# Mixture of experts in one layer of a two-block network: tokens of the first two expert pairs put in order by float32 products and a gather in place of products with bf16 parts

## The chip, the cores and the metric

The kernel runs on one core of a Trainium2 chip. The metric is the device time of that core in microseconds for one execution. Names of engines: PE is TensorE, DVE is VectorE, ACT is ScalarE, POOL is GpSimd, SP is SyncE, which here only issues DMA transfers.

## The reference, cut to what matters

The network has two blocks on 512 tokens of width 1024. The first block mixes tokens (`out_proj` is its last product and adds to X), then sends each token to two of 32 experts, then adds a small gated term; the second block has an attention mixer and an MLP. The part that the change touches is the second step of the first block:

```python
h = rmsnorm(x, g_ffn)
grp_logits = h @ w_grp                     # 4 groups, the best one is taken
exp_logits = h @ w_exp                     # 8 experts in each group, the best two of that group
gate = softmax(top two logits) * p_group
for each expert e:                         # on the tokens that chose e
    y = (silu(xb @ w1[e]) * (xb @ w3[e])) @ w2[e]
x = x + sum over a token's two experts of gate * y
```

Every expert has 1024x512 weights w1 and w3 and 512x1024 weights w2, in float32: 6 MB for an expert.

## The kernel before

**Pairs.** The 32 experts are worked off as 16 pairs. A pair has 128 places, 64 for each expert. `experts` runs over the pairs: the tokens of a pair stand turned in a tile xT (width on the partitions, places along the row), products L1090 and L1091 (one expert in each half of the array's columns) give w1's and w3's results (`up`, tile pa), then come the gate function, four transposes (pact), the products with w2 (py, L1179 and L1180) and the products that add the pair's result to X (pc, L1102). The next pair's w1 (`up(xs[0], True, turn)`) stands between a pair's w3 and its transposes, so that PE has work while DVE and ACT compute.

**Weights.** The weights come as 192 tiles of 1 MB by SP's queue (L670), 12 tiles for a pair. Each tile goes to a slot; the slots are used in turn, and a slot is loaded again when its products are done. At first 12 slots are loaded while `out_proj` and the router run: four `rg`, three `we`, the slot `hs[3]` and four of the ring; after the router seven more, three of `mg` and four of the ring. The slots `hs[1:3]` join the row after the first pair's w3, when the parts of X that they hold are no longer read. That makes 21.

**Order of tokens.** A pair's tokens are picked out by a matrix O of zeros and ones (token by place, bf16), which DVE makes from the places (L996, L997). There are two ways to xT:

- For the first two pairs the product of X and O gives xT directly (`add`, L1002, tile pxT). X is float32, so it is cut into three bf16 parts (`split3`, lines L175 to L183, in the slots `hs[0:3]`), and each of 4 token tiles x 8 blocks of the width takes three bf16 products: 96 for a pair. The first pair's products run while the router finishes (`first`): tiles 0 to 2 before, tile 3 last, since it needs the router's last places. The second pair's are done in two halves of 48 (`go`), one after the first pair's w1 and one after its w3.
- For the other pairs `fetch` multiplies O by the token's numbers and norms (tile pr, L1046), makes a list of rows from that on DVE (rsl, idx) and lets POOL gather these rows of X from DRAM (L1019, an indirect DMA from xd into xg, which lies in the slot `hs[0]` and is set to zero once by POOL, L1130). `go` then turns the gathered rows with eight transposes (L1033). The rows of X are written to xd by ACT's queue while the router runs.

**Router.** `Router.tile` runs for each of 4 token tiles beside the second half of `out_proj`: transposes of X (trp), logits (pl), a long row of small DVE operations for the best experts (lg to Mb), a count of places before this tile (pp), then slot and O. Tile 3's chain stands behind the last product of `out_proj`.

**Order of instructions.** A scheduler lists the instructions of each engine before the run, by priorities (`issue_after` holds back) and its own estimates. Engines then run their lists in order and wait for each other by semaphores.

Of the kernel before, what the change touches and what calls it, by code (L numbers as in the profile page):

```python
# [18 lines left out]
P = 128  # L19
# [667 lines left out]
def moe(N, a, mg, mixed):  # L687
# [4 lines left out]
    with ExitStack() as ctx:  # L692
# [53 lines left out]
        rtags = [(rg, "r%d" % i, 1) for i in range(4)]  # L746
        tags = [(we, "e%d" % i, 1) for i in range(3)]
        ring = [(N.ring, "w", RING)] * RING
        first = rtags[1:2] + rtags[:1] + rtags[2:] + tags + N.hs[3:] + ring[4:]
        W = Weights(N, a, first, [(0, NE)])  # L750
        H = [slot_tile(s, BF, (NT, D)) for s in N.hs[:3]]
        O = small("O", [P, 2, NT, P], BF)
        router = Router(N, mo, H, wr, c)

        def loaded():
            W.fetch(len(first))

        d = Dispatch(N, [(None, O[:, 0])] * 2, c, 0, (), H)
        router.d = d
        mixed(loaded, router.tile)  # L760
        W.free = mg[:3] + ring[:4]
# [22 lines left out]

        steps = {PLE_AT + i: lambda: next(pl.steps, 0) for i in range(1, 4)}
        steps.update({-1: where, PLE_AT: embed, PLE_AT + 4: rest})
        xs, pa = experts(N, bufs, c, W, 0, 14, [d], then=steps, H=H)

        over = [s for s in W.free if s not in ring][-3:]
        W.drop(over)  # L790
# [26 lines left out]
class Router:  # L817

    def __init__(self, N, mo, H, wr, c):
        self.N, self.mo, self.H, self.wr, self.c, self.pl = N, mo, H, wr, c, None

    def half(self, t, j):

# [12 lines left out]
            nc.tensor.matmul(self.pl[:, :36], lhsT=x[:, k * P:(k + 1) * P], rhs=self.wr[:, 4 * j + k, :],  # L838
                             start=j == 0 and k == 0, stop=j == 1 and k == 3)

    def parts(self, t, j):

        h = slice(j * 512, (j + 1) * 512)
        self.N.split3([x[:, t, h] for x in self.H], self.N.X[:, t, h], t == NT - 1 and j == 1)

    def tile(self, t):
        N, nc, c = self.N, self.N.nc, self.c
        if t == 0:
            self.half(0, 0)
            self.parts(0, 0)  # L850
        self.half(t, 1)
        nc.scalar.dma_start(c["xd"][t * P:(t + 1) * P, :], N.X[:, t, :])
        r = N.rnorm(t)
        if t == NT - 1:
            self.parts(t, 1)
            self.d.first((0, 1))
            self.d.first((2,))

        def st(name, n, dt=F32):
            return self.mo.tile([P, n], dt, tag=name, bufs=2, name=name)  # L860

        i32, slot, e12, q = (c[x] for x in ("i32", "slot", "e12", "q"))
        lg, m8, x8, Mb = (c[x][:, t, :] for x in ("lg", "m8", "x8", "Mb"))
        nc.vector.tensor_scalar(lg[:, :36], self.pl[:, :36], r, None, op0=OP.mult)
        i8, gs, pen, mk, j8 = st("i8", 8, U32), st("gs", 1), st("pen", 4), st("mk", NE), st("j8", 8, U32)
        nc.vector.max(m8, lg[:, 32:40])
        nc.vector.max_index(i8, m8, lg[:, 32:40])
        nc.vector.tensor_copy(gs, i8[:, 0:1])
        nc.vector.tensor_scalar(pen, i32[:, 0:4], gs, NEG, op0=OP.not_equal, op1=OP.mult)
        nc.vector.tensor_tensor(mk.rearrange("p (g e) -> p g e", g=4), lg[:, :NE].rearrange("p (g e) -> p g e", g=4),  # L870
                                pen[:, :, None].to_broadcast([P, 4, 8]), op=OP.add)
        nc.vector.max(x8, mk)
        nc.vector.max_index(j8, x8, mk)
        e = e12[:, :, t]
        nc.vector.tensor_copy(e, j8[:, 0:2])
        M1, jk, b = st("M1", NE), st("jkr", NE), st("sb", 2)
        nc.vector.tensor_scalar(M1, i32, e[:, 0:1], None, op0=OP.is_equal)
        nc.vector.scalar_tensor_tensor(Mb, i32, e[:, 1:2], M1, op0=OP.is_equal, op1=OP.add)
        pp = N.misc("pp")[:, :NE]
        for s in range(t):  # L880
            nc.tensor.matmul(pp, lhsT=c["two"], rhs=c["Mb"][:, s, :], start=s == 0, stop=False)
        nc.tensor.matmul(pp, lhsT=c["before"], rhs=Mb, start=t == 0, stop=True)
        nc.vector.tensor_scalar(b, e, 2.0 * CAP, None, op0=OP.mult)
        for i in range(2):
            nc.vector.scalar_tensor_tensor(jk, i32, e[:, i:i + 1], pp, op0=OP.is_equal, op1=OP.mult,
                                           accum_out=q[:, i, t:t + 1])

        nc.vector.scalar_tensor_tensor(b, q[:, :, t], 2.0 * CAP, b, op0=OP.is_ge, op1=OP.add)
        nc.vector.tensor_tensor(slot[:, :, t], b, q[:, :, t], op=OP.add)
        self.d.places(t, slot)  # L890
        if t < NT - 1:
            self.parts(t, 1)
        with N.tc.issue_after(self.d.last.ins):
            N.split3([c["r"][:, t, i:i + 1] for i in range(3)], r, True)
        if t < NT - 1:
            self.half(t + 1, 0)
            self.parts(t + 1, 0)


def gating(N, rt, c):  # L900
# [75 lines left out]
class Dispatch:  # L976
# [1 line left out]

    def __init__(self, N, bufs, c, pi, ts=range(NT), H=None):
        self.N, self.H, self.c, self.n, self.ps = N, H, c, 0, None
        self.pi = pi
        self.xT, self.O = bufs[pi % len(bufs)]
        self.two = len(bufs)
        sg = c["slot"]
        if pi:
            sg = N.tmp("sg", [P, 2, NT], tag="sg", bufs=2)
            N.nc.vector.tensor_scalar(sg, c["slot"], 4.0 * CAP * pi, None, op0=OP.subtract)
        for t in ts:  # L990
            self.places(t, sg)

    def places(self, t, sg):
        nc, iot = self.N.nc, self.c["iot"]
        o1 = self.c["mo"].tile([P, P], BF, tag="o1", bufs=2, name="o1")
        nc.vector.tensor_scalar(o1, iot, sg[:, 0, t:t + 1], None, op0=OP.is_equal)  # L996
        self.last = nc.vector.scalar_tensor_tensor(self.O[:, t, :], iot, sg[:, 1, t:t + 1], o1, op0=OP.is_equal,  # L997
                                                   op1=OP.add)

    def add(self, p, k, t, start=False):  # L1000
        for i in range(3):
            self.mm = self.N.nc.tensor.matmul(p, lhsT=self.H[i][:, t, every(k)], rhs=self.O[:, t, :],  # L1002
                                              start=start and i == 0, stop=t == NT - 1 and i == 2, skip_group_check=True)

    def out(self, p, k):
        N, nc = self.N, self.N.nc
# [17 lines left out]
    def go(self):  # L1024

        p = self.N.either("pxT")
        for i in range(4):
            k = self.n + i
            if self.H:
                for t in range(NT):  # L1030
                    self.add(p[:, i * P:(i + 1) * P], k, t, t == 0 and i == 0)
            else:
                self.mm = self.N.nc.tensor.transpose(p[:, i * P:(i + 1) * P], self.xg[:, every(k)], self.N.ident)  # L1033
        for i in range(4):
            self.out(p[:, i * P:(i + 1) * P], self.n + i)
        self.n += 4
        if self.n == KD and self.H:
            self.norm()
        return self

    def norm(self):
# [22 lines left out]
            self.norm()  # L1064


def experts(N, bufs, c, W, p0, p1, xs=None, pa=None, then={}, H=None):

# [38 lines left out]
    for pi in range(p0, p1):  # L1110
# [6 lines left out]
        nxt = None  # L1117
        if two and pi == 0:
            with N.tc.issue_after(xs[0].last.ins):
                xs.append(Dispatch(N, bufs, c, 1, H=H))  # L1120
            xs[1].go()
        x = xs.pop(0)
        pa.append(up(x))
        if left:
            with tc.issue_after(x.ups[3]):
                back(*left.pop())
        if two and pi == 0:
            xs[0].go()
            c["xg"] = slot_tile(N.hs[0], F32, (2, D))
            nc.gpsimd.memset(c["xg"], 0.0)  # L1130
            W.free += N.hs[1:3]
            xs.append(Dispatch(N, bufs, c, 2).fetch())
        if -1 - pi in then:
            then[-1 - pi]()
# [639 lines left out]
```

## Time and profile before

| what | us |
|---|---|
| median of 3 runs (1829.17 to 1829.71) | 1829.69 |
| the profiled execution | 1830.18 |
| its span, first to last instruction | 1828.5 |
| PE busy in the span | 1793.8 (98%) |
| DVE, ACT, POOL busy | 857.1, 586.7, 76.0 |

The experts run from 394.5 us to about 880 us of the span. The router, beside the second half of `out_proj`, runs from about 350 us to 394.5 us. Everything after that is the gated term of the first block and the second block. The page divides the span in 40 slices; PE's slices have a 9 (90% or more) from the second to the 39th. The clock granted to PE was 0.999 of full speed on average. The DMA share of a stretch is the mean busy share of the core's 16 DMA engines.

Products of float32 tiles take two records each in the trace where both operands are plain float32 (`sp`, `pl`); a transpose takes one.

### The profile page before, as it was taken

What the parts mean: (1) busy time and instruction counts of PE and PEld (TensorE: products, weight loads), DVE (VectorE), ACT (ScalarE), POOL (GpSimd) and SP (SyncE); (2) the same over time, 40 slices, a digit from 0 to 9 for tenths busy, and PEclk for the clock granted to TensorE, in tenths of its full rate; (3) what the DMA queues carried; (4) which work ended last, traced back from release to release, by engine and by line L of the source; (5) the groups of instructions that cost most, each with busy time, mean ns of one, the idle gap of its engine ahead of it and who ended that gap; (6) DMA issues with size and microseconds to landing.
All of it is one profiled execution on the core that took longest, in us unless ns stands there. A gap on an engine that the chain in (4) does not pass through costs nothing.

```text
span 1828.5 us, 20908 instructions
## 1 busy us (share of the span) xinstructions
PE 1793.8 (98%) x8425; PEld 1240.1 (68%) x8425; DVE 857.1 (47%) x1620; ACT 586.7 (32%) x953; POOL 76.0 (4%) x136
## 2 busy tenths in 40 slices
PE   7999999999999999999999999999999999999998
PEld 5777888864443444443677668787888888888886
DVE  6565433365545445324764557555224443333333
ACT  6453322322111112111755652424223432222221
POOL 1001000100000000000020010000000000000000
PEclk9999999999999999999999999999999999999999
DMA  5122223979999997999312021212233222332221
GB/s 191 47 92 90 78 93 97 354 258 424 423 423 423 423 409 303 424 423 374 131 36 91 24 73 46 92 36 81 82 103 130 87 72 94 96 104 99 92 92 46
DMA packets 117888, 322.60 MB, mean 176 GB/s; under 512 B 8797, under 2 KB 69393, under 8 KB 93720
## 3 DMA queue, kind: packets, MB, share of 16 engines
q1 hardware_dynamic: 115192, 315.46, 45.7%
q0 software_dynamic: 2016, 3.64, 0.5%
q10 hardware_dynamic: 576, 2.10, 0.3%
q8 instruction: 68, 1.11, 0.3%
q14 instruction: 36, 0.29, 0.0%
HBM read 320.68 MB, written 4.19 MB: 178 GB/s over the span
## 4 chain that ended last, share of the span: by engine, by line
PE 46%; issue 3%; ACT 2%; DVE 1%; POOL 1%; DMA 0%; POOLq 0%; DVEq 0%; ACTq 0%
PE acc L268 7%; PE acc L269 7%; PE acc L270 7%; PE pf L270 3%; PE pf L269 3%; PE pf L268 3%; PE pg L270 2%; PE pg L268 2%; PE pg L269 2%; PE psc L1605 2%; PE pu L270 1%; PE pu L268 1%; PE pu L269 1%; PE pa L1090 1%; PE po L1505 1%
## 5 line engine op out<-in xcount | busy, mean ns | idle before, releaser
L167 DVE TENSOR_TENSOR wlo<-wraw,whi 128x1024 fp32r<-128x1024 f32 (+2 forms) x165 | 226.5, 1384 | 350.9 <-PE pg L269 107.6
L165 ACT ACTIVATE whi<-wraw 128x1024 fp32r<-128x1024 f32 (+2 forms) x169 | 193.3, 1165 | 246.6 <-DMA wraw<-in_w_ff_dram 121.4
L268 PE MATMUL acc<-wh,whi 128*128 128x512 f32 (+1 forms) x448 | 170.7, 381 | 1.7 <-ACT fq L1442 1.0
L269 PE MATMUL acc<-wh,whi 128*128 128x512 f32 (+1 forms) x448 | 170.4, 380 | 0.0
L270 PE MATMUL acc<-wh,wlo 128*128 128x512 f32 (+1 forms) x448 | 169.9, 379 | 0.0
L268 PE MATMUL acc<-whi,wh 128*128 128x512 f32 x288 | 116.2, 404 | 0.6 <-ACT wh L165 0.4
L270 PE MATMUL acc<-whi,wh 128*128 128x512 f32 x288 | 114.9, 401 | 0.9 <-DVE wh L169 0.9
L269 PE MATMUL acc<-wlo,wh 128*128 128x512 f32 x288 | 114.9, 400 | 0.2 <-POOL wlo L167 0.2
L269 PE MATMUL pg<-wh,whi 128*128 128x512 f32 x256 | 101.5, 397 | 0.0
L268 PE MATMUL pg<-wh,whi 128*128 128x512 f32 x256 | 101.3, 396 | 0.0
L270 PE MATMUL pg<-wh,wlo 128*128 128x512 f32 x256 | 101.1, 395 | 0.0
L268 PE MATMUL pf<-whi,jh 128*128 128x512 f32 x256 | 101.1, 395 | 0.0
L269 PE MATMUL pf<-wlo,jh 128*128 128x512 f32 x256 | 101.1, 395 | 0.0
L270 PE MATMUL pf<-whi,jl 128*128 128x512 f32 x256 | 101.1, 395 | 0.0
L268 PEld LDWEIGHTS acc<-wh,whi 128*128 128x128 f32 x448 | 84.5, 189 | 21.5 <-issue 1.5
L269 PEld LDWEIGHTS acc<-wh,whi 128*128 128x128 f32 x448 | 84.5, 189 | 18.0 <-issue 1.8
L270 PEld LDWEIGHTS acc<-wh,wlo 128*128 128x128 f32 x448 | 84.5, 189 | 16.5
L1104 DVE TENSOR_TENSOR X<-pc,X 128x512 f32<-128x512 f32 x128 | 80.6, 684 | 15.2 <-PE pc L1102 14.3
L1090 PE MATMUL pa<-ww,wm 128*64 128x512 f32 x176 | 80.8, 599 | 0.3 <-PEq L803 0.3
L1091 PE MATMUL pa<-ww,wm 128*64 128x512 f32 x168 | 77.3, 599 | 0.0
L1102 PEld LDWEIGHTS pc<-y,OT 128*128 128x128 f32 x256 | 44.6, 188 | 41.7 <-issue 24.1
L1102 PE MATMUL pc<-y,OT 128*128 128x512 f32 x256 | 71.0, 411 | 0.3 <-DVE X L1104 0.2
(472 smaller groups left out, 3454.5 us busy)
## 6 DMA issues: line engine op xcount, KB each, us to landing
ww<-in_w_dram SPq DMA_DIRECT2D x71, 1024.0 KB
wraw<-in_w_in_dram SPq DMA_DIRECT2D x44, 1024.0 KB
wr<-in_w_dram SPq DMA_DIRECT2D x34, 1024.0 KB
wm<-in_w_dram SPq DMA_DIRECT2D x33, 1024.0 KB
wraw<-in_w_ff_dram SPq DMA_DIRECT2D x32, 1024.0 KB
wh<-in_w_dram SPq DMA_DIRECT2D x31, 1024.0 KB
we<-in_w_dram SPq DMA_DIRECT2D x23, 1024.0 KB
wraw<-in_w_out_dram SPq DMA_DIRECT2D x8, 1024.0 KB
```

The lines of the kernel that those rows point to most:

```text
L165: nc.scalar.activation(hi, src, AF.Copy, scale=scale)
L167: (pool or nc.vector).tensor_tensor(lo, src, f32v(hi), op=OP.subtract)
L268: mm(out, lhsT=lh, rhs=rh, start=start, stop=False, **kw)
L269: mm(out, lhsT=lh, rhs=rl, start=False, stop=False, **kw)
L270: mm(out, lhsT=ll, rhs=rh, start=False, stop=stop, **kw)
L1090: nc.tensor.matmul(p[0:64], lhsT=x.xT[:, kk, :64], rhs=wt[0][:, k, :], start=kk == 0, stop=kk == 7)
L1091: x.ups.append(nc.tensor.matmul(p[64:128], lhsT=x.xT[:, kk, 64:], rhs=wt[1][:, k, :], start=kk == 0, stop=kk == 7).ins)
L1102: nc.tensor.matmul(pc, lhsT=OT[:, t * P:(t + 1) * P], rhs=y[i], start=i == 0, stop=i == 1)
L1104: nc.vector.tensor_tensor(x, pc, x, op=OP.add)
L1505: nc.tensor.matmul(po[h * 64:(h + 1) * 64, i * P:], lhsT=v[:, i, (2 * c + h) * 64:(2 * c + h + 1) * 64], rhs=w[:, h, c0:c1], start=(i == N ...
L1605: nc.tensor.matmul(pl[:, cs], lhsT=fk[:, m, cs], rhs=fq[:, m, cs], start=True, stop=True)
```

## The change

The three bf16 parts of X and their operations (`parts`, `split3` on X) go. What takes their place:

- **First pair:** `places` also casts each tile's O to float32 (O0, one DVE copy for each of the four tiles), and `add` is one product of X and O0 in float32 in place of three: 32 products where 96 stood.
- **Second pair:** its Dispatch now calls `fetch` like those of the later pairs, behind the first pair's w1: product pr, list, gather. Its eight transposes (`go().go()`) stand behind the last product of the first pair's w3 (`issue_after(x.ups[-1])`). The third pair's `fetch` follows them.
- **Slots:** `hs[1:3]` hold no parts of X any more and are among the slots loaded first: 14 then, and all 21 from the beginning. The gather's buffer in `hs[0]` and its zeroing move to the beginning of `moe`.

```diff
-        first = rtags[1:2] + rtags[:1] + rtags[2:] + tags + N.hs[3:] + ring[4:]
+        first = rtags[1:2] + rtags[:1] + rtags[2:] + tags + N.hs[1:] + ring[4:]
         W = Weights(N, a, first, [(0, NE)])
-        H = [slot_tile(s, BF, (NT, D)) for s in N.hs[:3]]
+        c["xg"] = slot_tile(N.hs[0], F32, (2, D))
+        nc.gpsimd.memset(c["xg"], 0.0)
...
-        d = Dispatch(N, [(None, O[:, 0])] * 2, c, 0, (), H)
+        d = Dispatch(N, [(None, O[:, 0])] * 2, c, 0, (), N.tmp("O0").rearrange("p (t s) -> p t s", t=NT))
...
-    def parts(self, t, j):
-
-        h = slice(j * 512, (j + 1) * 512)
-        self.N.split3([x[:, t, h] for x in self.H], self.N.X[:, t, h], t == NT - 1 and j == 1)
...
+        if self.O0 is not None:
+            nc.vector.tensor_copy(self.O0[:, t, :], self.O[:, t, :])
 
     def add(self, p, k, t, start=False):
-        for i in range(3):
-            self.mm = self.N.nc.tensor.matmul(p, lhsT=self.H[i][:, t, every(k)], rhs=self.O[:, t, :],
-                                              start=start and i == 0, stop=t == NT - 1 and i == 2, skip_group_check=True)
+        self.mm = self.N.nc.tensor.matmul(p, lhsT=self.N.X[:, t, every(k)], rhs=self.O0[:, t, :], start=start,
+                                          stop=t == NT - 1, skip_group_check=True)
...
             with N.tc.issue_after(xs[0].last.ins):
-                xs.append(Dispatch(N, bufs, c, 1, H=H))
-            xs[1].go()
+                xs.append(Dispatch(N, bufs, c, 1).fetch())
         x = xs.pop(0)
         pa.append(up(x))
...
         if two and pi == 0:
-            xs[0].go()
-            c["xg"] = slot_tile(N.hs[0], F32, (2, D))
-            nc.gpsimd.memset(c["xg"], 0.0)
-            W.free += N.hs[1:3]
+            with tc.issue_after(x.ups[-1]):
+                xs[0].go().go()
             xs.append(Dispatch(N, bufs, c, 2).fetch())
```

The lists show it at three places. The first is PE between the last product of `out_proj` (acc) and the products of token tile 3; pp is the count of places (tile 3's are the last four), two and before are its matrices. Before, the products of tiles 0 to 2 are bf16 with a load of weights for each, and run on past the count for tile 2; this is a piece of that list:

```order
L1002 LDWEIGHTS wh_2387
L1002 MATMUL pxT<-O,wh_2387 128x128
L882 LDWEIGHTS before
L882 MATMUL pp<-Mb,before 128x32
L1002 LDWEIGHTS wh_2388
L1002 MATMUL pxT<-O,wh_2388 128x128
```

With the change, the same stretch in whole:

```order
L876 MATMUL pp<-Mb,before 128x32
L270 MATMUL acc<-whi,wm_1515 128x512
L994 MATMUL pxT<-O_2389,X 128x128 x4
L832 MATMUL trp<-ident,X 128x128 x4
L994 MATMUL pxT<-O_2389,X 128x128 x5
L839 MATMUL pl<-wr,xr 128x36 x4
L994 MATMUL pxT<-O_2389,X 128x128 x15
L875 LDWEIGHTS two
L875 MATMUL pp<-Mb,two 128x32
```

The 72 bf16 products between the last acc and tile 3's count have become 24 float32 ones, and the count for tile 2 now stands ahead of the last acc.

The second place is PE from the first pair's w3 to the second pair's w1 (L1090 and L1091 before, L1075 and L1076 now). Before, 48 bf16 products stand in front of w3 and 48 more behind it; this is the piece at w3's end:

```order
L1091 MATMUL pa<-wh_2540,wm_3040 64x512
L1090 MATMUL pa<-we_2538,wm_3040 64x512
L1091 MATMUL pa<-wh_2540,wm_3040 64x512
L1002 LDWEIGHTS wh_2386
L1002 MATMUL pxT<-O,wh_2386 128x128
L1002 LDWEIGHTS wh_2387
```

With the change (wh_2386 is the gather's buffer; the four pr between w1 and w3, not shown, feed the gather's list):

```order
L1076 MATMUL pa<-wh_2540,wm_2960 64x512
L1021 MATMUL pxT<-ident,wh_2386 128x128 x8
L1032 LDWEIGHTS O
L1032 MATMUL pr<-r,O 128x6
...
L917 MATMUL pm<-ident,qm 1x128
L1075 MATMUL pa<-wh_2542,wm_2960 64x512
L957 MATMUL sp<-ident,slot 128x128 x8
```

Eight transposes of the gathered rows stand where 48 products stood, and nothing but four pr stands between w1 and w3.

The third place is SP's list at the end of the mixer, a piece of the difference: the slots `hs[1]` and `hs[2]` are loaded (wh_2540 and wh_2542 here are `hs[1]` and `hs[2]` now, and wh_2540 was `hs[3]` before), the first of them ahead of the third tile of `out_proj`'s weights.

```order
-L252 DMA wraw<-in_w_out_dram 128x4x512 x4
+L252 DMA wraw<-in_w_out_dram 128x4x512 x2
 L670 DMA wh_2540<-in_w_dram 128x2048
+L252 DMA wraw<-in_w_out_dram 128x4x512 x2
+L670 DMA wh_2542<-in_w_dram 128x2048
```

One weight tile now stands before the last two tiles of `out_proj`'s weights, and one behind them.

## Rows read from the trace of the kernel before

**Rows 1.** The page, its part on engines: busy us, share of the span, instructions.

```profile
PE 1793.8 (98%) x8425; PEld 1240.1 (68%) x8425; DVE 857.1 (47%) x1620; ACT 586.7 (32%) x953; POOL 76.0 (4%) x136
```

**Rows 2.** Stretches: us, PE, PEld, DVE, ACT, POOL busy; granted clock, DMA share, GB/s.

```profile
390.00:400.00 10.00, 8.26 (x77) 4.62 (x77) 8.03 (x44) 2.87 (x6) 0.00 (x0) 1.00 0.31 112
...
420.00:520.00 100.00, 100.00 (x476) 41.36 (x476) 52.88 (x151) 16.66 (x33) 4.43 (x4) 1.00 1.01 423
```

**Rows 3.** Waits of PE, 400 to 900 us, longest of five: us in total, times, longest.

```profile
PE pact L1157 <- DVE ms L1150: 0.9, 1, 0.9
...
```

**Rows 4.** PE in order of time, first pair: start, us, line, operation, records, [idle before].

```profile
394.54 0.64 PE L1090 MATMUL pa<-wr,wm 128*64 128x512 f32 x1
...
401.56 2.87 PE L1002 MATMUL pxT<-O,wh 128*128 128x128 bf16 x48
...
411.38 2.87 PE L1002 MATMUL pxT<-O,wh 128*128 128x128 bf16 x48
...
414.49 1.07 PE L1090 MATMUL pa<-ww,wm 128*64 128x512 f32 x2
415.49 2.05 PE L966 MATMUL sp<-ident,slot 128*128 128x128 f32 x16
417.38 1.11 PE L966 MATMUL sp<-ident,gates 128*128 128x128 f32 x8
```

**Rows 5.** PE in order of time, a later pair's transposes and its pr.

```profile
427.50 1.23 PE L1033 MATMUL pxT<-ident,wh 128*128 128x128 f32 x8
428.57 0.24 PE L1046 MATMUL pr<-r,O 128*128 128x6 bf16 x4
```

**Rows 6.** DVE in order of time, behind the same pr.

```profile
428.29 1.20 DVE L1010 TENSOR_SCALAR wm<-pxT,gp 128x128 f32<-128x128 f32 x3 [2.46 <-PE pxT L1033]
...
430.05 0.15 DVE L1017 TENSOR_SCALAR idx<-rsl 128x1 int32<-128x1 f32 x1
```

**Rows 7.** POOL in order of time, the gather behind that pr.

```profile
430.48 1.11 POOL L1019 DMA_INDIRECT wh<-xd,idx  x1 [12.66 <-DVE O L997]
```

**Rows 8.** Line L1019 over the whole span (14 gathers).

```profile
DMA to landing us min/median/max: 7.8/8.1/10.9
```

**Rows 9.** Line L1019 from 410 to 420 us alone, the first gather.

```profile
DMA to landing us min/median/max: 9.5/9.5/9.5
```

**Rows 10.** The page, its part on DMA queues: packets, MB, share.

```profile
q0 software_dynamic: 2016, 3.64, 0.5%
```

**Rows 11.** PE in order of time, the router's end.

```profile
383.36 0.39 PE L270 MATMUL acc<-whi,wm 128*128 128x512 f32 x1
383.59 0.97 PE L1002 MATMUL pxT<-O,wh 128*128 128x128 bf16 x14
384.53 0.66 PE L831 MATMUL trp<-ident,X 128*128 128x128 f32 x4
385.02 0.94 PE L1002 MATMUL pxT<-O,wh 128*128 128x128 bf16 x14
385.98 1.08 PE L838 MATMUL pl<-wr,xr 128*128 128x36 f32 x8
...
389.83 1.50 PE L1002 MATMUL pxT<-O,wh 128*128 128x128 bf16 x24 [1.52 <-DVE O L997]
391.17 0.18 PE L882 MATMUL pp<-Mb,before 128*128 128x32 bf16 x1
...
393.10 1.50 PE L1002 MATMUL pxT<-O,wh 128*128 128x128 bf16 x24 [1.74 <-DVE O L997]
```

**Rows 12.** DVE in order of time, the end of tile 3's chain.

```profile
392.70 0.35 DVE L997 SCALAR_TENSOR_TENSOR O<-iot,slot,o 128x128 bf16<-128x128 f32 x1
```

**Rows 13.** SP in order of time: start, us in which the group was issued, tile.

```profile
317.54 2.52 SPq L252 DMA_DIRECT2D wraw<-in_w_out_dram  x2
...
398.24 4.22 SPq L670 DMA_DIRECT2D wr<-in_w_dram  x3
```

**Rows 14.** ACT in order of time, the next cut of `out_proj`'s weights behind those loads.

```profile
328.47 1.92 ACT L165 ACTIVATE whi<-wraw 128x2048 fp32r<-128x2048 f32 x1 [2.92 <-PE pu L269]
```

More of the change, by code (lines that the diff above doesn't have):

```diff
@@ L748, in moe @@
         ring = [(N.ring, "w", RING)] * RING
-        first = rtags[1:2] + rtags[:1] + rtags[2:] + tags + N.hs[3:] + ring[4:]
+        first = rtags[1:2] + rtags[:1] + rtags[2:] + tags + N.hs[1:] + ring[4:]
         W = Weights(N, a, first, [(0, NE)])
-        H = [slot_tile(s, BF, (NT, D)) for s in N.hs[:3]]
+        c["xg"] = slot_tile(N.hs[0], F32, (2, D))
+        nc.gpsimd.memset(c["xg"], 0.0)
         O = small("O", [P, 2, NT, P], BF)
-        router = Router(N, mo, H, wr, c)
+        router = Router(N, mo, wr, c)
         def loaded():
             W.fetch(len(first))
-        d = Dispatch(N, [(None, O[:, 0])] * 2, c, 0, (), H)
+        d = Dispatch(N, [(None, O[:, 0])] * 2, c, 0, (), N.tmp("O0").rearrange("p (t s) -> p t s", t=NT))
         router.d = d
@@ L786, in moe @@
         steps.update({-1: where, PLE_AT: embed, PLE_AT + 4: rest})
-        xs, pa = experts(N, bufs, c, W, 0, 14, [d], then=steps, H=H)
+        xs, pa = experts(N, bufs, c, W, 0, 14, [d], then=steps)
         over = [s for s in W.free if s not in ring][-3:]
@@ L817, with __init__ @@
 class Router:
-    def __init__(self, N, mo, H, wr, c):
-        self.N, self.mo, self.H, self.wr, self.c, self.pl = N, mo, H, wr, c, None
+    def __init__(self, N, mo, wr, c):
+        self.N, self.mo, self.wr, self.c, self.pl = N, mo, wr, c, None
     def half(self, t, j):
@@ L849, in tile @@
             self.half(0, 0)
-            self.parts(0, 0)
         self.half(t, 1)
@@ L854, in tile @@
         if t == NT - 1:
-            self.parts(t, 1)
             self.d.first((0, 1))
@@ L890, in tile @@
         self.d.places(t, slot)
-        if t < NT - 1:
-            self.parts(t, 1)
         with N.tc.issue_after(self.d.last.ins):
@@ L896, in tile @@
             self.half(t + 1, 0)
-            self.parts(t + 1, 0)
 def gating(N, rt, c):
@@ L976, with __init__ @@
 class Dispatch:
-    def __init__(self, N, bufs, c, pi, ts=range(NT), H=None):
-        self.N, self.H, self.c, self.n, self.ps = N, H, c, 0, None
+    def __init__(self, N, bufs, c, pi, ts=range(NT), O0=None):
+        self.N, self.O0, self.c, self.n, self.ps = N, O0, c, 0, None
         self.pi = pi
@@ L1028, in go @@
             k = self.n + i
[L1029 to L1033, printed above, removed]
+            self.mm = self.N.nc.tensor.transpose(p[:, i * P:(i + 1) * P], self.xg[:, every(k)], self.N.ident)
         for i in range(4):
@@ L1036, in go @@
         self.n += 4
-        if self.n == KD and self.H:
-            self.norm()
         return self
@@ L1064, in first, with experts @@
             self.norm()
-def experts(N, bufs, c, W, p0, p1, xs=None, pa=None, then={}, H=None):
+def experts(N, bufs, c, W, p0, p1, xs=None, pa=None, then={}):
     nc, tc = N.nc, N.tc
```

## The prediction

> **What bounds the kernel now.** I read the page's engine part first: PE is busy for 1793.8 of 1828.5 us, every other engine for less than half [rows 1]. So a change counts only where it takes PE time away or opens a gap on PE. Next the stretches and the waits of the experts: from 400 to 900 us PE's five waits sum to 2.6 us, the longest is 0.9, and none is on a DMA [rows 3], although the DMA engines run at a share of 1.01 through that time [rows 2]. The weights are thus a close second, but landed tiles are in stock and nobody waits for them. A tile of 1 MB takes 1.049 MB / 423 GB/s = 2.48 us there. Before that, from 390 to 400 us, the DMA share is 0.31: with 19 slots full, SP has nothing to load until 398.24 [rows 2, 13]. Last the router's end and the first pair in order of time: PE waits there twice for DVE's O (1.52 and 1.74 us) [rows 11], then runs w1 (394.54 to 401.56, 7.02 us), 48 bf16 products, w3 (the same 7.02), 48 products and some small ones, until the second pair's w1 starts at 414.49 [rows 4]. I call the start of the first pair's w1 S; from S to the second pair's w1 it is 19.95 us now.
>
> **Part 1: the first pair's products.** In the place of 96 bf16 products stand 32 float32 ones. 24 bf16 take 1.44 to 1.50 us (1.50 by the row) [rows 11], 0.06 us each. A float32 product of the same 128x128x128 shape is sp: 16 records, 8 products, 415.49 to 417.38, 0.236 us each [rows 4]. So 96 x 0.06 = 5.8 us become 32 x 0.236 = 7.6 us, 1.8 us more work. What of it is on the path? The last acc of `out_proj` ends near 383.59. Behind it now come 4 products (0.94), four trp (0.49, from 384.53 to 385.02), 5 products (1.18), four pl (0.91) and 15 products (3.54): 383.59 + 7.06 = 390.65. Then tile 3's count pp, which stands at 391.17 before [rows 11]. DVE may be ready for it at about the same time or earlier, since the cuts of X leave its list. So pp comes 0.5 us sooner. From pp to the products of tile 3 it is 1.93 us before [rows 11]; O0 adds one small DVE copy, which I put at 0.25 us from O's own 0.35 [rows 12]. Then 8 float32 products take 1.89 where 24 bf16 took 1.44. S moves by -0.5 + 0.25 + 0.45 = **+0.2 us**. The two waits are eaten by the larger products; that is why 1.8 us of work costs so little. Bounds: -0.7 if the lighter DVE list brings the chain forward as well, +1.8 if nothing of the added work is absorbed.
>
> **Part 2: the second pair's 96 products go.** From S the new list is w1 7.02, four pr 0.17, w3 7.02, eight transposes 1.07, four pr 0.17, and pm with the last copy to xT, about 0.5. The eight transposes and the four pr are read from a later pair: 427.50 to 428.57, and 0.24 with the drain of the last [rows 5]. The sum is 15.95 us, if the gathered rows are there in time, against 19.95: **-4.0 us**.
>
> **Part 3: the gather's wait.** Here the change adds a wait. PE comes to the transposes at S + 7.02 + 0.17 + 7.02 = S + 14.2. The list of rows can only be made behind the pr that now follow w1, at S + 7.02. In a later pair POOL's gather starts 1.91 us after its pr [rows 5, 7], but DVE had three copies of pxT (1.20 us) ahead of rsl there and idx only at 430.05 [rows 6]. In the new place no such copies stand ahead, only parts of O for the third pair; I take 1.5 us. The gather is thus issued at S + 8.5. It lands 7.8 to 10.9 us after its issue, 8.1 in the median of 14 [rows 8]; the first one of the kernel took 9.5 [rows 9]. I take 9.5, because the new gather will be the first of the kernel, in the same stretch, beside the same loads. It lands at S + 18.0, and PE waits for 18.0 - 14.2 = **3.8 us**. With 1.3 and 7.8 the wait is 1.9, with 1.9 and 10.9 it is 5.6. Behind the transposes PE's whole list is queued: the pr for the third pair, the second pair's w1 and all that follows; nothing else of PE's stands ahead to fill the gap. DVE's and ACT's copies of pxT wait with it, and POOL's next gather waits for pr.
>
> By the Trainium skill ("DMA: Bandwidth & Descriptors", section "Anatomy of one DMA — SWDGE (gpsimd) path") a DMA of this path takes about 2.0 us and its bytes at 436 GB/s. The trace has 3.64 MB for the 14 gathers, 0.26 MB each [rows 10], so the rule would make 2.6 us (an estimate from that page), and there would be no wait; the case is rival A below, which stands on its own rows. The trace does not agree while the weights are streaming: 7.8 us at least [rows 8].
>
> **Part 4: two more slots at first.** Two more tiles load while the mixer and the router run, 2 x 2.48 = 5.0 us of DMA, and they fill most of the idle stretch before 398.24 [rows 2, 13]. The stock of landed tiles rises by two. I price it at 0, because PE doesn't wait for weights [rows 3]; the work that hides the loads is PE's own. One load moves ahead of the third tile of `out_proj`'s weights on SP's queue. That tile would be issued at 317.54 and lands 2.5 us later now; the next cut of these weights is at 328.47 [rows 13, 14], so some 5 us of cover are left. If the cover were gone it would cost up to 2.48. The zeroing of the gather's buffer moves to POOL's list before the router's constants, where POOL is idle. The cuts of X were on DVE, ACT and POOL beside `out_proj`, under PE's products: 0.
>
> **Sum.** Against the profiled execution of 1830.18 us (span 1828.5): +0.2 - 4.0 + 3.8 = 0.0. That execution lies 0.5 us over the median of the runs, which is what the time will be held against: 1829.69 + 0.0, rounded to **1829.7 us**. The order behind the second pair's w1 is the old one but for a handful of places in the fourth pair, so every microsecond saved or lost here passes to the end, as PE has no gap to swallow it.
>
> **Rivals.**
>
> *A: the gather is in time.* If it lands within 5.7 us of its issue (S + 8.5 to S + 14.2) there is no wait: +0.2 - 4.0 = -3.8, 1825.9 us. For it: 0.26 MB is little. Against: all 14 gathers beside the weight stream took 7.8 us or more [rows 8], and the DMA engines will be loading at that moment, since w1's four slots come free from S + 3.7 on (398.24 in this trace) [rows 13]. With more slots filled, that stretch is not emptier than before. Chance 0.10.
>
> *B: weights do bind.* If PE's rate in the experts was set by the DMA share of 1.01 [rows 2] and the trace hides the wait in PE's modelled busy time, two tiles of stock are worth 5.0 us: 1829.7 - 5.0 = 1824.7. Against: PE's waits name no DMA [rows 3]. Chance 0.04.
>
> *C, slower: the gather queues behind weights.* The two extra preloads and w1's four freed slots stand in the DMA queues ahead of it. If the two add in full, it lands 9.5 + 5.0 = 14.5 us after issue and PE waits 8.5 + 14.5 - 14.2 = 8.8 us: +0.2 - 4.0 + 8.8 = +5.0, 1834.7 us. It decides from a landing of 13.2 us on, where the sum passes +3.7. For it: the first gather's 9.5 and one of 10.9 show that landing depends on what is queued [rows 8, 9]. Against: at 390 to 400 us the queue is nearly empty, and two tiles fit into that [rows 2]; and no gather came near 13. Chance 0.11.
>
> *D: the float32 products don't hide.* All 1.8 us of added work comes on the path in front of S: 1829.7 + 1.6 = 1831.3. The two waits of 1.52 and 1.74 us [rows 11] speak against it, the in-order list of PE for it. Chance 0.12.
>
> **How the numbers follow.** The forecast has 0.63, A 0.10, B 0.04, C 0.11, D 0.12. A measurement of this kernel can tell about 0.2%, 3.7 us, from no change. The forecast and D lie within it; A stands at its edge, so half of it is "faster" and half "same": faster 0.04 + 0.05 = 0.09, same 0.63 + 0.12 + 0.05 = 0.80, slower 0.11. The forecast's own range goes from -2.8 (S -0.7, wait 1.9) to +3.4 (S +1.8, wait 5.6): 1826.9 to 1833.1. The wanted range takes A in at the low end and leaves out B and C: 1825.8 to 1833.1.
>
> **What would show it right or wrong.** Right: S within 1 us of 394.5; four pr directly behind w1, w3 directly behind them; one wait of PE of 2 to 5.6 us on the transposes, released by the gather; the second pair's w1 near 414.5; no other new wait; 390 to 400 us with a DMA share near 0.8; and after 420 us the same periods of pairs. Wrong: no such wait (A), a wait over 8 us (C), pairs that come faster than before (B), or S at 396 or later (D). A wait on `out_proj`'s weights near 350 us would mean that the load on SP's queue was not covered.

## The result and the profile after

The changed kernel takes 1840.68 us in the median (6 runs, 1838.53 to 1842.09), the kernel before 1829.61 (6 runs, 1828.76 to 1829.71). The ratio is 1.006, with a 95% interval of 1.0047 to 1.0073: slower by some 11 us. The forecast was 1829.7, with a range to 1833.1; the measured time lies above it.

The page of the changed kernel, its part on engines (busy us, share, instructions):

```profile
span 1840.3 us, 20640 instructions
...
PE 1801.9 (98%) x8305; PEld 1246.3 (68%) x8305; DVE 851.3 (46%) x1609; ACT 577.2 (31%) x938; POOL 75.0 (4%) x136
```

PE's busy time has grown by 8.1 us against [rows 1], although 120 instructions fewer stand in its row. The rest of the 11.8 us by which the span grew are waits. PE's waits from 300 to 950 us (us in total, times, longest):

```profile
PE pa L1075 <- PEq L804: 3.1, 1, 3.1
PE pxT L1021 <- DMA wh<-xd,idx: 2.4, 1, 2.4
PE pxT L994 <- DVE O L991: 2.0, 1, 2.0
```

The second is the new wait for the gather. The third is the old wait for O, once in place of twice. The first, at a branch far from the change, was 0.3 us before. PE in order of time, from the end of `out_proj` to the second pair's w1 (start, us, line, operation, records, [idle before]):

```profile
383.51 0.48 PE L270 MATMUL acc<-whi,wm 128*128 128x512 f32 x1
383.83 1.90 PE L994 MATMUL pxT<-O,X 128*128 128x128 f32 x8
385.57 0.60 PE L832 MATMUL trp<-ident,X 128*128 128x128 f32 x4
386.01 2.49 PE L994 MATMUL pxT<-O,X 128*128 128x128 f32 x10
388.34 0.98 PE L839 MATMUL pl<-wr,xr 128*128 128x36 f32 x8
389.15 7.24 PE L994 MATMUL pxT<-O,X 128*128 128x128 f32 x30
396.23 0.23 PE L875 MATMUL pp<-Mb,two 128*128 128x32 bf16 x3
396.31 0.18 PE L876 MATMUL pp<-Mb,before 128*128 128x32 bf16 x1
...
398.50 4.05 PE L994 MATMUL pxT<-O,X 128*128 128x128 f32 x16 [1.95 <-DVE O L991]
...
402.48 0.64 PE L1075 MATMUL pa<-wr,wm 128*64 128x512 f32 x1
...
419.17 1.85 PE L1021 MATMUL pxT<-ident,wh 128*128 128x128 f32 x8 [2.40 <-DMA wh<-xd,idx]
...
421.26 1.83 PE L1075 MATMUL pa<-wh,wm 128*64 128x512 f32 x2
423.03 2.05 PE L957 MATMUL sp<-ident,slot 128*128 128x128 f32 x16
```

The row of 30 records is 15 products: from 389.15 to the next work at 396.23 they take 7.08 us, 0.472 us each, where the sum had 0.236. The first pair's w1 starts at 402.48, 7.94 us later than before [rows 4].

Where the 11.8 us of the span arise, by the starts of the same work in both traces (the changed kernel's profiled execution is its slowest, 1842.09 us, 1.4 above its median):

| stretch | before, us | after, us | difference |
|---|---|---|---|
| start to the first pair's w1 | 394.54 | 402.48 | +7.94 |
| to the second pair's w1 | 19.95 | 18.78 | -1.17 |
| to the first pair's w2 | 14.25 | 15.02 | +0.77 |
| 13 more pairs (w2 to w2) | 391.69 | 390.65 | -1.04 |
| over the branch, to the next w2 | 27.89 | 33.51 | +5.62 |
| to the end | 980.18 | 979.86 | -0.32 |

Two places make the loss: the products in front of the first pair, and the branch.

### The profile page after: what moved, and what is told of

Its sections match the earlier page's. It is cut to its first block, busy times and chain, and to the rows that moved or that the text cites. A ratio compares the mean times of both kernels' runs of the same rounds, so it can differ in the third digit from the quotient of the medians.

```text
span 1840.3 us, 20640 instructions
## 1 busy us (share of the span) xinstructions
PE 1801.9 (98%) x8305; PEld 1246.3 (68%) x8305; DVE 851.3 (46%) x1609; ACT 577.2 (31%) x938; POOL 75.0 (4%) x136
## 4 chain that ended last, share of the span: by engine, by line
PE 47%; issue 3%; ACT 2%; DVE 1%; POOL 1%; DMA 0%; POOLq 0%; DVEq 0%; ACTq 0%
PE acc L268 7%; PE acc L269 7%; PE acc L270 7%; PE pf L270 3%; PE pf L269 3%; PE pf L268 3%; PE pg L269 2%; PE pg L268 2%; PE pg L270 2%; PE psc L1587 2%; PE pu L269 1%; PE pu L268 1%; PE pu L270 1%; PE pa L1075 1%; PE po L1487 1%
## 5 line engine op out<-in xcount | busy, mean ns | idle before, releaser
L1076 PE MATMUL pa<-ww,wm 128*64 128x512 f32 x192 | 90.9, 615 | 0.0
L1075 PE MATMUL pa<-ww,wm 128*64 128x512 f32 x160 | 74.1, 598 | 0.0
```

The lines of the kernel that those rows point to most:

```text
L1075: nc.tensor.matmul(p[0:64], lhsT=x.xT[:, kk, :64], rhs=wt[0][:, k, :], start=kk == 0, stop=kk == 7)
L1076: x.ups.append(nc.tensor.matmul(p[64:128], lhsT=x.xT[:, kk, 64:], rhs=wt[1][:, k, :], start=kk == 0, stop=kk == 7).ins)
```

## The experiments

Two questions stood open: why the float32 products take twice their price, and how two slots for weights, or anything else in the change, can cost 5.6 us at a branch 400 us later. Each run below was taken beside runs of the kernel before (medians 1828.9 to 1829.0). Beside the changed kernel that median was 1829.6, so where a run is set against the changed kernel's median of 1840.68, 0.6 to 0.7 us of the difference need not come from the edit.

**e1: neighbouring columns.** The first pair's products take 128 columns of X that lie side by side.

```diff
-        ... lhsT=self.N.X[:, t, every(k)], rhs=self.O0[:, t, :] ...
+        ... lhsT=self.N.X[:, t, k * P:(k + 1) * P], rhs=self.O0[:, t, :] ...
```

> The changed kernel with one edit: the first pair's float32 products take 128 neighbouring columns of X as the loaded operand in place of every fourth column (so xT holds the widths in another order than the weights do: the result is not the reference's). Theory: the loads of every fourth float32 are what is slow (0.33 us against 0.19, one product 0.47 us against 0.236 of sp). Then a load is about 0.19 us, 24 products take about 5.7 us in place of 11.1, the first pair's w1 starts at 395 to 397 us in place of 402.5, and the median is 6 to 8 us below the changed kernel's 1840.7: 1833 to 1835. Rival: a float32 product with X as the loaded operand takes this time whatever its columns; then w1 starts at 402.5 and the time stays at 1840.7. The waits at the gather (2.4 us) and at the branch (3.1 us) are not touched by either.

Measured: 1833.49 us (10 runs, 1830.61 to 1835.03), 7.2 below the changed kernel. The loads and products of this line, changed kernel (instructions, then duration in ns min/median/max, first and last start):

```profile
L994 PEld LDWEIGHTS pxT<-O,X x64: 308/329/332, 383.6 to 402.0; 128*128 128x128 f32 x64
```

The same line in e1, and below it PE in order of time:

```profile
L994 PEld LDWEIGHTS pxT<-O,X x64: 186/192/193, 384.2 to 395.1; 128*128 128x128 f32 x64
```

```profile
387.78 3.59 PE L994 MATMUL pxT<-O,X 128*128 128x128 f32 x30
391.21 0.23 PE L875 MATMUL pp<-Mb,two 128*128 128x32 bf16 x3
...
393.47 2.05 PE L994 MATMUL pxT<-O,X 128*128 128x128 f32 x16 [1.95 <-DVE O L991]
...
395.46 0.64 PE L1075 MATMUL pa<-wr,wm 128*64 128x512 f32 x1
```

The products are the same in number and shape; only the addresses of the loaded operand differ. A load falls from 329 to 192 ns, 15 products from 7.08 to 3.43 us (387.78 to the next work at 391.21), and w1 starts at 395.46, 7.02 us earlier. The rival, that float32 products of X are that slow whatever their columns, falls. The branch still makes PE wait 2.7 us here. The sign of it stood in the trace of the kernel before, in rows that I hadn't looked at. Loads for transposes, a single record each, of neighbouring columns (L831) and of every fourth one (L1033):

```profile
L831 PEld LDWEIGHTS trp<-ident,X x32: 137/141/224, 359.1 to 384.8; 128*128 128x128 f32 x32
```

```profile
L1033 PEld LDWEIGHTS pxT<-ident,wh x112: 195/212/220, 427.5 to 820.1; 128*128 128x128 f32 x112
```

The Trainium skill ("SBUF — State Buffer", section "Door 1: The DMA port swizzle (why `[64,N]` ≈ `[32,N]`)") says that reads that go to another 16-byte line with each access pay for it. Every fourth float32 is 16 bytes on; these runs agree (329 against 192 ns), while the bf16 parts with the same step of four elements, 8 bytes, took 113 ns a load, not far from the 96 ns of bf16 loads from neighbouring columns (O for pr).

**e2: the two slots join late.** As in the kernel before, behind the first pair's w3.

```diff
-        first = rtags[1:2] + rtags[:1] + rtags[2:] + tags + N.hs[1:] + ring[4:]
+        first = rtags[1:2] + rtags[:1] + rtags[2:] + tags + N.hs[3:] + ring[4:]
...
                 xs[0].go().go()
+            W.free += N.hs[1:3]
```

> The changed kernel with one edit: the two slots hs[1:3] join only after the first pair's w3, as in the kernel before, so 12 in place of 14 are loaded first. Theory on the branch (the test for overflow, line 804, where PE waits 3.1 us in the changed kernel and 0.3 before): SP holds its loads there until all earlier ones have landed; with two tiles more in stock it starts the next ones before PE has fetched its code behind the branch, and the fetch waits behind 5 MB of weights. Without the two, SP starts again later than PE's branch: PE's wait falls to under 1 us, the clock stays at 1.00 there, and the median falls by about 5.6 us to 1835. Rival: the wait comes from the code itself (another length, another place) and stays at 3 us; then 1840.7. Second rival: the two slots are worth something in the experts; then pairs come slower and the time rises to 1843 or more. The first pair's w1 stays at 402.5 us in every case.

Measured: 1837.58 us (4 runs, 1836.53 to 1837.64), 3.1 below the changed kernel's median and 4.7 in the profiled span. The 5.6 us show in the profile at the branch (27.95 us from w2 to w2 there, in place of 33.51); in the medians only about half of it was gained. The second rival holds for a small part: the 13 pairs take 391.31 us here, 0.7 more than with the two slots early. The w1 of the first pair starts at 402.74, 0.3 later. PE's wait at the branch:

```profile
PE pa L1075 <- PEq L804: 0.4, 1, 0.4
```

So the two slots are what brings the wait at the branch; the rival with the code's length falls, since the code is the same but for one line. PE's own queue and SP's, changed kernel: how long PE's jump took (ns, start us), and SP's next loads (start, us in which the group was issued):

```profile
L804 PEldq COMPARE_BRANCH  x1: 6607/6607/6607, 840.2 to 840.2; - x1
```

```profile
837.49 0.34 SPq L670 DMA_DIRECT2D wh<-in_w_dram  x1
837.89 2.94 SPq L670 DMA_DIRECT2D ww<-in_w_dram  x5
```

The same in e2:

```profile
L804 PEldq COMPARE_BRANCH  x1: 3487/3487/3487, 840.9 to 840.9; - x1
```

```profile
842.11 0.35 SPq L670 DMA_DIRECT2D wh<-in_w_dram  x1
842.52 2.91 SPq L670 DMA_DIRECT2D ww<-in_w_dram  x5
```

PE's jump in the kernel before:

```profile
L803 PEldq COMPARE_BRANCH  x1: 3852/3852/3852, 833.7 to 833.7; - x1
```

SP waits at the branch until its earlier loads have landed, and then issues six tiles in a row. In the changed kernel that starts 2.7 us ahead of PE's jump, in e2 1.2 us behind it. During a jump of 6.6 us PE first runs what it has in its queue and then stands for 3.1 us; the clock granted behind that wait falls to its lower level (1.2 GHz). Stretches of the changed kernel (us, PE, PEld, DVE, ACT, POOL busy; granted clock, DMA share, GB/s):

```profile
842.00:844.00 2.00, 2.00 (x10) 0.43 (x6) 0.00 (x0) 0.00 (x0) 0.00 (x0) 1.00 1.01 422
844.00:846.00 2.00, 0.06 (x2) 0.00 (x0) 0.00 (x0) 0.00 (x0) 0.00 (x0) 1.00 1.05 434
...
848.00:852.00 4.00, 4.00 (x12) 1.35 (x10) 3.77 (x12) 0.00 (x0) 0.00 (x0) 0.50 1.01 418
```

The step from one pair of w3's products to the next there is 0.85 us in place of 0.43 (847.13 to 853.03 for seven): 2.9 us more. With the wait's 3.08 - 0.32 = 2.8 that is the 5.6 us of the table.

**e3: no branch.** The block under the test for overflow, a loop for experts with more tokens than places, is left out (here and in e8; these inputs don't enter it).

```diff
-        with tc.If(n > 0):
-            with tc.For_i(0, n, 1):
-            ...
```

> The changed kernel without the block under the test for overflow (the loop for experts with more tokens than places, which these inputs don't enter) and so without the branch. Theory: PE's wait of 3.1 us at the branch and the half clock behind it (847 to 853 us) go, 5.6 us together: 1835. Rival: that wait is really for the weights behind the branch, which the profile puts down to the branch; then PE waits about as long for a DMA there, and the time stays within 1 us of 1840.7.

Measured: 1828.83 us (10 runs, 1828.07 to 1829.98), 11.9 below the changed kernel. The wait is gone and no other came in its place, but the gain is twice what was expected: without the block the rest of the program takes less time too (6 us less behind the experts, and 2 us less before the first pair). PE's products stand in the same order there, up to 836 us and from 880 us on; why they take less time is not shown. e8 is the control for that.

**e8: the kernel before without the branch.**

> The kernel before without the block under the test for overflow and without its branch (it leaves out the loop for experts with more tokens than places, which these inputs don't enter). e3 fell by 12 us without it, more than the 5.6 us of the wait and the half clock at the branch, so the branch must cost in other ways as well. Theory: SP's drain of all loads and the order forced around the branch cost both kernels some 6 us, and the changed kernel 5 to 6 us more: this one is at 1822 to 1824. Rival: the branch costs the kernel before next to nothing (PE waits 0.3 us there); then 1828 to 1829.

Measured: 1821.85 us (4 runs, 1821.67 to 1822.24), 7.1 below the kernel before. So leaving the block out gains some 7 us in both kernels, and in the changed one 11.9 - 7.1 = 4.8 us more (4.2 with each held against the kernel before that ran beside it). The 7 us are not a cost at the branch: PE waits 0.3 us there, PE's products stand in the same order up to 830 us and from 867 us on, and PE is busy for 8.2 us less (1785.6), before the first pair and behind the experts above all. Without the block the change costs 1828.83 - 1821.85 = 7.0 us, close to what e1 gave for the columns (7.2, or 6.6 beside the kernel before). Both runs leave out a part that other inputs need, so neither is a version to use.

**e4: the second pair's part alone.** First pair as in the kernel before; the gather's buffer and the two slots come when the first pair's products are done.

```diff
             with N.tc.issue_after(xs[0].mm.ins):
                 pa.append(up(xs[0]))
+        if two and pi == 0:
+            c["xg"] = slot_tile(N.hs[0], F32, (2, D))
+            nc.gpsimd.memset(c["xg"], 0.0)
+            W.free += N.hs[1:3]
...
-                xs.append(Dispatch(N, bufs, c, 1, H=H))
-            xs[1].go()
+                xs.append(Dispatch(N, bufs, c, 1).fetch())
...
-            xs[0].go()
+            with tc.issue_after(x.ups[-1]):
+                xs[0].go().go()
```

> The kernel before with the second pair's part of the change alone: the first pair keeps its products with bf16 parts of X, the second pair is gathered and turned behind the first's w3; the gather's buffer is set to zero and hs[1:3] join when the first pair's products are done. Theory: the first pair's w1 starts at 394.5 as before; w1, w3 and the turn take 16 us without 96 products; PE waits 2 to 4 us for the gather, the clock falls to 0.5 for about 3 us behind that and costs 1 to 1.5 us; the second pair's w1 starts at 413.5 to 415.5 (414.5 before). Since the two slots' loads start at 394.5, the stock is larger than before and the branch costs some 5 us as in the changed kernel: 1832 to 1835. If the branch costs nothing: 1828 to 1830. Rival (the float32 products alone made the time of the changed kernel, all else is small): 1825 to 1827, four microseconds below before.

Measured: 1831.59 us (10 runs, 1830.16 to 1833.66); against the kernel before 1.0014 (1.0004 to 1.0024). PE's wait:

```profile
PE pxT L1033 <- DMA wh<-xd,idx: 3.7, 1, 3.7
```

The second pair's part takes 4 us of products out and puts a wait of 3.7 us and 3 us at half clock in, as the prediction's parts 2 and 3 had it but for the clock. The branch costs nothing here (0.3 us of wait, a jump of 3.4 us): SP's next loads start at 835.96, PE's jump at 835.6. I had expected it to cost 5 us, since the slots join early; what counts is not the stock but which of the two starts first. The time still lies above the 1828 to 1830 expected for a branch that costs nothing. In the profile the second pair's w1 starts at 414.49 as before, w2 comes 1.0 us later, and the 13 pairs take 0.9 us longer; what makes the rest is not shown.

**e5: the number of tiles ahead of the branch.** A test of that alone, with both slots in the first list.

```diff
-AHEAD = 9
+AHEAD = 11
```

> The changed kernel with one number changed: 11 in place of 9 weight tiles are issued ahead of the branch (line 804). Both slots stay in the first list. Theory on the branch: what counts is whether SP starts its next 5 MB before or after PE's jump asks for its code. In the runs so far: SP starts again 0.4 to 1.6 us after PE's branch and the jump takes 3.4 to 3.9 us (the kernel before, e2, e4), or 2.3 to 2.4 us ahead of it and the jump takes 6.2 to 6.6 us (changed kernel, e1). With two tiles more ahead of the branch SP's drain ends about 5 us later, at 841 to 843, behind PE's branch at 840.2: the jump takes 3.4 to 5.5 us, PE's wait there falls from 3.1 to 0.3 to 2 us, and the median is 2 to 5.5 us below 1840.7. Rival: the two slots cost something of themselves, or the jump's length comes from the code; then the jump stays above 6 us and the time within 1 us of 1840.7.

Measured: 1834.58 us (5 runs, 1834.36 to 1837.55), 6.1 below the changed kernel, where 2 to 5.5 was expected. PE's jump takes 3.8 us, its wait 0.3, and SP's earlier loads have landed only at 843.2, behind PE's jump at 841.6. The rival, that the two slots cost something of themselves, falls.

**e6: the changed kernel with an earlier gather.** The second pair's `fetch` stands ahead of the call for the first pair's w1, so its pr fall within w1.

> The changed kernel with the second pair's list of rows asked for earlier: its four pr stand within the first pair's w1 in place of behind it, so the gather starts 3 to 4 us sooner. Theory: PE's wait for the gather (2.4 us) goes, and with it the half clock of 419 to 422.6 us; the second pair's w1 comes 3 to 4 us sooner, and the median falls to 1836.5 to 1838.5, with the wait at the branch as it is in the changed kernel (the branch and SP's start both move). Rival: the gather lands by the weight loads ahead of it and not by its issue; then the wait stays above 1.5 us and the time at 1840.

Measured: 1836.81 us (4 runs, 1835.80 to 1839.11), 3.9 below the changed kernel. PE has no wait for the gather any more; it was issued at 407.89 and landed 5.8 us later. The wait at the branch stays (2.7 us), with SP's loads at 834.85 and the jump at 837.8.

**e7: e4 with the earlier gather.**

> e4 (first pair by bf16 parts as before, second pair gathered, slots free when the first pair is put in order) with the pr within the first pair's w1. Theory: no wait for the gather and no half clock, so the second pair's w1 starts at about 410.5 in place of 414.5, and every pair behind it 4 us sooner than before until the branch. What the branch does then is open: PE comes to it at about 831 us, when the earlier loads have not landed yet; if the jump takes 3.5 us the time is 1825 to 1826, 3 to 4 us below the kernel before, with 5 to 6 us it is 1827 to 1829. Rival: the gather still makes PE wait; then it is e4's 1831.6.

Measured: 1827.26 us (11 runs), 0.9996 of the kernel before (0.9987 to 1.0005), in two groups: seven runs from 1825.97 to 1828.77 and four from 1830.50 to 1831.94. The profiled run is of the upper group. SP's loads start at 831.42, PE's jump at 831.9 and takes 6.1 us. Half a microsecond decides, and it seems to fall to either side from run to run; of the lower group there is no profile.

**e9 and e10: e7 with 10 and with 11 tiles ahead of the branch.**

> e7 with 10 in place of 9 weight tiles issued ahead of the branch. e7's runs fall into two groups, 1826.0 to 1827.3 and 1828.8 to 1831.9; in the profiled one, of the upper group, SP starts its next 5 MB at 831.4 us, 0.5 us ahead of PE's branch at 831.9, and the jump takes 6.1 us. Theory: one tile more ahead of the branch moves SP's start behind PE's branch (833.5 to 835) and PE's jump falls into the stretch in which the DMA engines run dry: jump 3.4 to 4 us, PE's wait 0.3 us, all runs in the lower group: 1825.5 to 1827, 2 to 3.5 us below the kernel before. Rival: the two groups have another cause (the start of the program); then they stay, and the median is 1827 to 1829.

> e7 with 11 tiles ahead of the branch. SP's drain then ends at 836 or later, and the DMA engines are still busy with earlier weights when PE's jump asks for its code at 831.9. Theory, if only SP's start counts: jump 3.4 to 4 us, 1825.5 to 1827 as with 10. If every load in the queues holds the code up, those ahead of the branch as well as those behind it (ACT's jump in the kernel before, asked for at 828.1 us with the DMA engines at a share of 1.0, took 5.3 us): jump 4.5 to 6 us, PE's wait 1 to 2.5 us, 1827 to 1830.

Measured: 1826.28 us (11 runs, 1825.15 to 1828.08) and 1825.93 us (11 runs, 1824.99 to 1828.20); against the kernel before 0.9986 (0.9977 to 0.9995) and 0.9983 (0.9974 to 0.9992). The upper group is gone, and PE's jump takes 3.6 and 3.35 us in the two profiles. That fits an upper group that came from the branch, though e7's lower group has no profile to show it. e10's second pair starts 3.5 us earlier than before [rows 4], with no wait ahead of it; PE in order of time:

```profile
409.64 1.24 PE L1033 MATMUL pxT<-ident,wh 128*128 128x128 f32 x8
410.71 0.24 PE L1046 MATMUL pr<-r,O 128*128 128x6 bf16 x4
410.81 0.27 PE L926 MATMUL pm<-ident,qm 128*1 128x128 f32 x1
411.01 1.07 PE L1090 MATMUL pa<-ww,wm 128*64 128x512 f32 x2
```

In e10 the DMA engines still run at a share of 0.97 (830 to 832 us) when PE's jump asks at 831.4, yet it takes 3.35 us. So loads that are nearly through (a share of 0.61 from 832 to 834 us) don't hold it up, and the rival in e10's expectation falls for them. ACT's jump of 5.3 us, on which that rival rested, stays unexplained. e10 is faster than both kernels: 3.1 us below the kernel before.

All kernels at the branch. SP's next loads is the start of the first load that it issues behind its drain:

| kernel | SP's next loads, us | PE's jump asked, us | jump took, us | PE's wait, us |
|---|---|---|---|---|
| before | 834.1 | 833.7 | 3.85 | 0.3 |
| e2 | 842.1 | 840.9 | 3.49 | 0.4 |
| e4 | 836.0 | 835.6 | 3.39 | 0.3 |
| e5 | 843.6 | 841.6 | 3.81 | 0.3 |
| e9 | 833.8 | 831.2 | 3.59 | 0.3 |
| e10 | 836.6 | 831.4 | 3.35 | 0.7 (for DVE's jump) |
| changed | 837.5 | 840.2 | 6.61 | 3.1 |
| e1 | 830.5 | 833.3 | 6.21 | 2.7 |
| e6 | 834.9 | 837.8 | 6.27 | 2.7 |
| e7 | 831.4 | 831.9 | 6.11 | 2.6 |

Where SP starts behind the jump it takes 3.35 to 3.85 us, where SP starts ahead of it 6.1 to 6.6. The Trainium skill ("Runtime: NRT & Kernel Launch", section "Instruction fetch mechanics") says that a taken branch out of the code at hand has to wait for a DMA that brings the page of its target. The trace has a DMA that fits it: in each of these ten jumps one packet of queue q8, kind instruction, starts. In the changed kernel it starts between 844.4 and 844.6 us, in the kernel before between 834.7 and 834.9 (the queue's row in these two stretches: packets, MB, share):

```profile
q8 instruction: 1, 0.02, 30.3%
```

```profile
q8 instruction: 1, 0.02, 43.6%
```

In the six short jumps this packet starts 1.0 to 1.1 us behind the asking, in the four long ones 3.7 to 4.3 us, and the jump ends 1.3 to 1.4 us behind the packet's end in all ten. So the jump is long because its code is fetched late, while the tiles that SP has just issued are loading. The packet doesn't wait for all of them: six tiles take 6 x 2.48 = 15 us.

## Why the prediction was wrong, point by point

**The bound** was read rightly: PE sets the time, and the pairs between the first and the branch keep their steps (13 of them 390.65 against 391.69 us), with two tiles more in stock. Nobody waits for weights there, and rival B is out.

**Part 1 is the step that failed first.** The price of a float32 product was taken from sp, 0.236 us. That row's loaded operand is one column repeated, while the first pair's is every fourth column of X. The products take 0.472 us: 24 of them 11.2 us with their gaps left out (1.74, 2.33 and 7.08) in place of 5.66, the last eight 3.88 in place of 1.89. The sum's own chain, with these two terms, gives 5.5 + 2.0 = 7.5 us more, so w1 at 402.2; it was 402.48. Rival D named the place but had the same price, and so only +1.6.

**Part 2** held: w1 and w3 take 7.02 us each, and without its wait the stretch to the second pair's w1 is 18.78 - 2.40 = 16.38 us, against 15.95. The transposes alone were 0.57 longer, 1.64 in place of 1.07 at a granted clock of 0.50 to 0.71; the small products behind them were a little shorter than in the sum.

**Part 3** held in its mechanism and was priced too high: the gather was issued at 410.83, 8.35 us behind w1's start (8.5 in the sum), and landed 8.2 us later (9.5 in the sum); the wait was 2.4 in place of 3.8. In e4 landing took 8.9 and the wait was 3.7. Asked for within w1, 2.9 us sooner (e6), it landed after 5.8 us, so 5.3 us sooner, at a DMA share of 0.82 in that time. So the landing depends on when a gather is asked for, which the sum's fixed 9.5 left out. The prediction's estimate of 2.6 us from the Trainium skill ("DMA: Bandwidth & Descriptors", section "Anatomy of one DMA — SWDGE (gpsimd) path") doesn't hold beside the weight stream, and rival A, a landing within 5.7 us, is out. The clock behind the wait was left out of the sum. Changed kernel, the stretches around the two waits:

```profile
396.00:398.00 2.00, 0.55 (x9) 0.44 (x8) 1.29 (x8) 0.00 (x0) 0.00 (x0) 1.00 0.00 0
...
399.00:402.00 3.00, 3.00 (x14) 3.00 (x15) 0.70 (x2) 0.37 (x1) 0.00 (x0) 0.50 0.00 0
...
420.00:422.00 2.00, 2.00 (x11) 1.24 (x10) 1.30 (x6) 0.93 (x3) 0.00 (x0) 0.50 1.02 430
```

It cost little at the first: the loads of X pace the products there, 0.24 us a record at half clock and 0.236 at full. Behind the gather it cost 0.6 us on the transposes and the 0.77 us up to w2: the next two products, the first of the second pair's w1, take 1.77 us up to sp (421.26 to 423.03) in place of 1.00 [rows 4]. e6, without the gather's wait and the half clock behind it, has w2 2.4 us sooner (433.86 against 436.28).

**Part 4 is the step that failed second.** Two more slots were priced at 0 since PE doesn't wait for weights. They speed the 13 pairs up by 0.7 to 1.0 us at most (390.65 against 391.31 in e2 and 391.69 before), but they move SP against PE, and at the branch that costs 5.6 us in the profiled run (e2, e5). The sign named for them, a DMA share near 0.8 from 390 to 400 us, did not come either: it was 0.25. The sentence that every microsecond passes to the end as PE has no gap to swallow it looked only at waits that exist; the branch is a place where a shift makes one. Its row in the waits of before was counted among the five and passed over as small:

```profile
PE pa L1090 <- PEq L803: 0.3, 1, 0.3
```

Rival C, the slower one, was about a gather behind weights; what came behind weights was code.

**The size of the sum.** 7.5 for part 1 and 5.6 at the branch less the 1.4 of part 3 make 11.7 above the forecast's own basis; 11.1 was measured in the medians.

**Open:** why the clock falls behind some waits of 2 us or more and not behind others (e6 waited 2.7 us at the branch, and the clock stayed at 1.00), why loads that SP has just issued hold the code's packet up and loads nearly through don't, and why PE's products far from the branch take less time in e3 and e8, in the same order.

## What to carry to other kernels

Take the price of a product from a row whose loaded operand has the same step in memory, not only the same shape; the weight loads' own rows (PEld) show it where PE's busy time doesn't. A branch in a stream of weights is a race between the code that the jump needs and the loads that a DMA queue issues at the same moment: look at who starts first, and set the number of loads ahead of the branch so that the jump wins. Ask for a gather as early as its list can be made, within the product before if need be: the second pair's took 7.9 to 8.9 us to land where it was asked for behind w1, and 5.4 to 5.9 us where it was asked for within w1 (e6, e7, e9 and e10).

## What the runs showed of the hardware that was not expected

- A load of 128x128 float32 takes 192 ns from neighbouring columns and 329 ns from every fourth one (e1 against the changed kernel); for transposes it is 141 against 212 ns, and for bf16 96 against 113 ns.
- PE's jump behind the branch takes 3.35 to 3.85 us, or 6.1 to 6.6 when SP starts its next weight tiles 0.5 to 3 us ahead of it; the packet with its code then starts 3.7 to 4.3 us behind the asking in place of 1.0. In e7, where the two are 0.5 us apart, the runs fall into two groups, with medians nearly 5 us apart.
- Within or behind PE's waits of 1.9 to 3.7 us the granted clock fell to 0.50 for about 3 to 7 us in most cases; behind one wait each in e1 (1.95), e3 (2.05), e6 (2.7) and e10 (1.9) it stayed at 1.00. Before the change, waits of 1.52 and 1.74 us [rows 11] left it at 1.00.
